# Value projection of a hybrid decoder trunk: a weight's two parts as one moving operand of 512 columns

## The chip, the cores and the metric

The kernel runs on one core of a Trainium2 chip. The metric is the device time of one execution in microseconds; a smaller time is better. The times below are medians over several executions, and the profile belongs to one execution of its own. Engines are named as in the profile: PE is TensorE's matmul and PEld its weight load, DVE is VectorE, ACT is ScalarE, POOL is GpSimd, and SP is SyncE, which issues most transfers.

## The reference

One layer of a decoder is computed on 1024 rows of 1024 columns: an RMS norm, two token mixers side by side (a gated linear recurrence, RG-LRU, and a gated linear attention with 8 heads, HGRN2), an output projection with residual, a second norm, a squared-ReLU MLP with residual, and a last norm. The part that matters here is the value projection of the second mixer:

```python
h = rms_norm(x, norm_mix[l])
proj = h @ w_in
xa, ga, q, f, v, g, m_a, m_b = jnp.split(proj, SPLIT_POINTS, axis=-1)
...
vf = v.astype(jnp.float32).reshape(B_, S_, HG_HEADS, HG_DV)
o = rms_norm(hgrn2_chunkwise(qf, kf, log_f, vf), hg_norm)
...
x = x + hybrid_mixer(h, lower_bounds[l], ...)
h = rms_norm(x, norm_mlp[l])
x = x + jnp.square(jax.nn.relu(h @ w_up[l])) @ w_down[l]
```

## The kernel before

**Two parts of a number.** Products keep close to float32 precision because each operand is split in two: a rounded part (names ending in H) and the rest (names ending in L), both in the fp32r format. A cast on ACT makes the rounded part (L87), a subtraction on DVE the rest (L92). A product is then three matmuls into one PSUM bank, H by H, H by L and L by H; `mm3` issues them (L146 to L150).

**Stages.** The mixers work in eight stages: 2 chunks c of 512 rows times 4 pairs p of heads, named c0 p0 to c1 p3. `stage(i)` projects what pair i needs from the normalised rows: xa (the recurrence's input, with its convolution), q, f, and the recurrence's gates (`rg_lru`). The value projection of a pair is made one stage later: `stage(i+1)` begins with `v_of(i+1)`, which runs `v_steps` for pair i (L521 to L538). At the same time `hgrn(i)` (from L664) makes the scores and states of pair i. The two are interleaved by hand: `hgrn` calls `go(n)`, which lets the following stage go n steps on. The numbers come from the tables GO, GO_FIRST and GO_SECOND_HALF (L36 to L38). In most stages 22 steps come first (16 of them values), then the score product of level 1 (`pt1`, 32 small matmuls out of q1 and kk), 2 steps, that of level 2 (`pt2`, out of qa and kb), 2 steps, and that of level 8 (`pt8`). These three are recorded at L678; in the orders below they are sc1, sc2 and sc8.

**A value projection.** `v_steps` makes for each of four row tiles (tt, 128 rows) a sum over eight contraction tiles k. The rows' transposed parts hh and hl are the stationary operand of 128 by 128, and 256 columns of the weight are the moving operand. The result, 128 by 256 in PSUM, is copied to SBUF by ACT (L535) and is read much later (`po`, L870, and `pkv`, L845). After row tile 0, `between` runs the tail of the recurrence of the pair: its elementwise products and two scans along time on DVE (L627 to L631). The first pair's values, v_00, are made elsewhere (`first_norm`, L382 to L397).

**PSUM banks.** Eight banks are given out by tag in turn: "pj" has four, "sc" two, "hg" two. Row tiles 0, 1 and 3 of the values take a "pj" bank, row tile 2 an "sc" bank. The turn of "sc" in a stage is: the gates' second half (pr and pi), the values' row tile 2, sc1, sc2, and later the product sc64. So sc2 takes the bank of row tile 2. In the turn of "pj" the three value tiles are followed by xa's two banks and q's two; xa's second bank takes that of row tile 0, and q's two take those of row tiles 1 and 3.

**Weights.** `next_w` hands out weights in a fixed sequence. A weight's H and L are two tiles of 128 by 1024 of the tag "w", of which there are six: three weights are held at a time. `split_w` fills them; on a weight's second use the rest is loaded back from DRAM. `pair` in the MLP takes tiles of the same ring.

**Order of the work.** PE's matmuls of the mixers are kept in program order (`pin`). On DVE and ACT the scheduler sets the order of the instructions from its own estimates, except where the code says otherwise (`keep`, `high_priority`).

**After the mixers.** The output projection follows (`out_proj`), then the MLP, as block products with fewer multiplications by a plan of sums (PLAN, from L1059). Between its up and down halves DVE forms sums of weight blocks (L1089 to L1098), rests (L92) and the squared-ReLU input (L1530).

Of the kernel before, what the change touches and what calls it, by code (L numbers as in the profile page):

```python
# [11 lines left out]
F32R = mybir.dt.float32r  # L12
U8 = mybir.dt.uint8
AF = mybir.ActivationFunctionType
ALU = mybir.AluOpType
# [3 lines left out]
P = 128  # L19
# [26 lines left out]
def trunk(ctx: ExitStack, tc: tile.TileContext, x, wts, mlp, pv, gains, mask_f, mask_u, out):  # L46
    nc = tc.nc
    V, A, G, PE = nc.vector, nc.scalar, nc.gpsimd, nc.tensor

    const = ctx.enter_context(tc.tile_pool(name="const", bufs=1))  # L50
    wp = ctx.enter_context(tc.tile_pool(name="wp", bufs=1))
# [30 lines left out]
    def keep(ins):  # L82
        if in_order[0]:
            tc.keep_in_program_order(ins)
# [14 lines left out]
    def load_w(i):  # L99
        raw = raw_tile(f"raw{i}")  # L100
        nc.sync.dma_start(raw, seq[i])
        return raw

    def split_w(i, raw):
        if i < n_mix + 3:
            h, lo = (wp.tile([P, 1024], F32R, tag="w", name=f"w{q}{i}", bufs=6) for q in "HL")
        else:
            h, lo = (kept[0].tile([P, 1024], F32R, tag=f"k{q}{i - n_mix}", name=f"w{q}{i}") for q in "HL")
        at = pair_tiles[i] if i < len(pair_tiles) else None
        with tc.high_priority(400):  # L110
            if at in rests:
                A.copy(h, raw)  # L112
                nc.sync.dma_start(lo.bitcast(F32), rests[at])
                return h, lo
            split(raw, h, lo)
        if at is not None and at in pair_tiles[i + 1 :]:
            rests[at] = dram.tile([P, 1024], F32, tag=f"rest{at}", name=f"rest{at}")
            nc.sync.dma_start(rests[at], lo.bitcast(F32))
        return h, lo
# [10 lines left out]
    def get_w(i, ahead=2):  # L130
        fill_w(i + ahead + 1)
        return ready.pop(i)

    used = [0]

    def next_w():
        used[0] += 1
        return get_w(used[0] - 1)
# [3 lines left out]
    def pin(ins):  # L142
        if pinned[0]:
            tc.keep_in_program_order(ins)

    def mm3(o, ah, al, bh, bl, first, last, goes_on=False):  # L146
        how = {"skip_group_check": True} if goes_on else {}
        pin(PE.matmul(o, ah, bh, start=first, stop=False, **how))  # L148
        pin(PE.matmul(o, ah, bl, start=False, stop=False, **how))  # L149
        pin(PE.matmul(o, al, bh, start=False, stop=last, **how))  # L150
# [75 lines left out]
    def mt(tag, name, shape=(P, T), dt=F32, bufs=1):  # L226
        return m.tile(list(shape), dt, tag=tag, name=name, bufs=bufs)
# [65 lines left out]
    def first_norm():  # L293
# [73 lines left out]
        ws, pv = {}, {}  # L367

        def w_high(i):
            ws[i] = tuple(wp.tile([P, 1024], F32R, tag="w", name=f"w{q}{i}", bufs=6) for q in "HL")  # L370
            keep(A.copy(ws[i][0], xraws[i]))

        def w_low(i):
# [6 lines left out]
        v = mt("v", "v_00", (P, 4, 256))  # L380
# [139 lines left out]

    def v_steps(c, p, got, between):  # L521
        v = mt("v", f"v_{c}{p}", (P, 4, 256))
        w = [next_w(), next_w()]
        for tt in range(4):
            pp = bank("sc" if tt == 2 else "pj", f"pv_{c}{p}_{tt}")
            for k in range(8):
                hh, hl = kt(hT[c], k)
                cut = slice(tt * P, (tt + 1) * P)
                cols = slice((k % 4) * 256, (k % 4 + 1) * 256)
                wh, wl = w[k // 4]  # L530
                mm3(pp[:, :256], hh[:, cut], hl[:, cut], wh[:, cols], wl[:, cols], k == 0, k == 7)
                if k % 2:
                    if k < 7:
                        yield
            A.copy(v[:, tt, :], pp[:, :256])  # L535
            between(tt)
            yield
        got["v"] = v  # L538
# [540 lines left out]
    def quad_steps(i, pools, raws=raw_tile, minus=False):  # L1079

        ops = ops_w[i] = {}
        s = []

        def sums(behind=None):
            ra, rb = (r.rearrange("p (a b) -> p a b", a=2) for r in raw_q[i])
            a11, a21, a12, a22 = ra[:, 0, :], ra[:, 1, :], rb[:, 0, :], rb[:, 1, :]
            s.extend(raws(f"s{i}{h}") for h in range(2))
            sa, sb = (r.rearrange("p (a b) -> p a b", a=2) for r in s)
            ins = V.tensor_tensor(out=sa[:, 0, :], in0=a21, in1=a22, op=ALU.add)  # L1089
            if behind is not None:  # L1090
                how = mybir.DependencyInfo(mybir.DependencyClass.NoSync, mybir.DependencyReason.DATA)
                tc.add_manual_dep(ins.ins, behind.ins.name, how, reason="sums")
            if minus:
                V.scalar_tensor_tensor(sa[:, 1, :], sa[:, 0, :], -1.0, a11, op0=ALU.mult, op1=ALU.subtract)
            else:
                V.tensor_tensor(out=sa[:, 1, :], in0=sa[:, 0, :], in1=a11, op=ALU.add)
            V.tensor_tensor(out=sb[:, 0, :], in0=a21, in1=a11, op=ALU.add)  # L1097
            V.tensor_tensor(out=sb[:, 1, :], in0=a12 if minus else sa[:, 1, :], in1=sa[:, 1, :] if minus else a12, op=ALU.subtract if minus else ALU.add)  # L1098

        def single(behind=None):  # L1100
            t = pools[0].tile([P, 2, 512], F32R, tag="w1", name=f"wA11{i}", bufs=2)
            split(raw_q[i][0][:, 0:512], t[:, 0, :], t[:, 1, :], behind)
            ops["A11"] = (t[:, 0, :], t[:, 1, :])

        def pair(src, names):
            def go(pool=None, tag=None, bufs=None):
                if pool:
                    t = pool.tile([P, 2, 1024], F32R, tag=tag, name=f"w{names[0]}{i}", bufs=bufs)
                    h, lo = t[:, 0], t[:, 1]
                else:  # L1110
                    h, lo = (pools[1].tile([P, 1024], F32R, tag="w", name=f"w{names[0]}{i}{q}", bufs=6) for q in "HL")
                split(src(), h, lo)
                for j, o in enumerate(names):
                    cols = slice(j * 512, (j + 1) * 512)
                    ops[o] = (h[:, cols], lo[:, cols])

            return go

        return {
            "sums": sums,  # L1120
            "a": single,
            "b": pair(lambda: s[0], ("s1", "s2")),
            "c": pair(lambda: s[1], ("s3", "s4")),
            "d": pair(lambda: raw_q[i][1], ("A12", "A22")),
        }
# [9 lines left out]
    for o in ("t1", "n2", "T4", "T3"):  # L1135
        pool = np_ if o in ("t1", "n2") else tp
# [315 lines left out]
    for part in range(2):  # L1452
# [4 lines left out]
        for hf in range(2):  # L1457
            pp = {tt: bank("pj", f"po1{hf}{tt}") for tt in tts}
# [3 lines left out]
            for n, (j, those) in enumerate(turn):  # L1462
                if n == 4:
                    first_weights()
                wh, wl = out_w[4 * hf + j]
                for k in range(2):
                    ku = 2 * j + k
                    yh, yl = ykt1(part, ku)
                    cols = slice(k * 512, (k + 1) * 512)
                    for tt in those:  # L1470
                        cut = slice((tt % 2) * P, (tt % 2 + 1) * P)
# [3 lines left out]
            for tt in tts:  # L1475
                cols = slice(hf * 512, (hf + 1) * 512)
# [176 lines left out]
    for kb in range(n_kb):  # L1653
        last = kb + 1 == n_kb
        qs = order[2 * kb : 2 * kb + 2]
        for half in range(2):
# [8 lines left out]
            for step, (bk, wo, uo), prs in [  # L1665
# [3 lines left out]
                for i, q in enumerate(qs):  # L1669
                    wh, wl = ops_w[QUADS + q][wo]  # L1670
                    uh, ul = u_ops[q][uo]
                    for pr in prs:
                        if first and i == 0:
                            banks[bk, pr] = bank(BANK[bk], f"d{bk}{kb}{pr}")
                        cut = slice(pr * P, (pr + 1) * P)
                        mm3(banks[bk, pr], uh[:, cut], ul[:, cut], wh, wl, first and i == 0, i == 1, not first)
                for pr in prs:
                    _, ci, cj, op = ADDS[step]
# [92 lines left out]
```

## Time and profile before

| | us |
|---|---|
| median of 3 runs | 1538.94 (1538.2 to 1539.3) |
| the profiled execution | 1538.52 |
| its span, first to last instruction | 1536.7 |
| PE busy | 1522.4 (99%) |
| DVE busy | 1149.0 (75%) |
| ACT busy | 804.6 (52%) |
| POOL busy | 153.6 (10%) |
| mean granted PE clock | 0.998 |

A row of a timeline reads: start in us from the span's start, duration in us, engine, line, operation, output <- inputs (by the program's names, without buffer numbers), shapes, and in brackets the idle time of the engine just before it with what ended it. A row with "x64" is 64 instructions drawn together. A row of waits reads: the waiting engine, tile and line, what it waited for, and then us in total, the number of times, and the longest. A row of a group gives the shortest, median and longest duration in ns, and the first and last start. Matmuls overlap one another, so their pace is read from the distance of their starts.

### The profile page before, as it was taken

The page shows a single profiled execution, that of the slowest core. Times are in us where ns is not written, and L with a number is a line of the kernel's source. Part 1 is how long each engine was busy: PE and PEld are TensorE (multiplying, and loading weights), DVE is VectorE, ACT ScalarE, POOL GpSimd, SP SyncE. Part 2 cuts the span into 40 slices and gives each one's busy share as a digit, 9 for nine tenths or more (in the row PEclk, how much of TensorE's full clock was granted, in tenths as well). Part 3 has the DMA queues.
Part 4 walks back from the last instruction along what each step waited for, and adds up shares of the span by engine and source line. Part 5 has one row for each costly group of instructions (what it writes and reads, how often), then busy time and mean ns, then how long its engine had stood idle before and what let it go on. Part 6 is the DMA issues. An engine that isn't in the chain of part 4 may idle for free. (4 is left out here: it accounts for less than half of the span.)

```text
span 1536.7 us, 23202 instructions
## 1 busy us (share of the span) xinstructions
PE 1522.4 (99%) x9085; PEld 1275.2 (83%) x9085; DVE 1149.0 (75%) x1656; ACT 804.6 (52%) x1341; POOL 153.6 (10%) x188
## 2 busy tenths in 40 slices
PE   9999999999999999999999999999999999999997
PEld 7878988889889888888888888888888788888886
DVE  6798695485675838786856578888888898888877
ACT  6646757567567335454533447666666721111115
POOL 1022210232624600000000000000000000000000
PEclk9999999999999999999999999999999999999999
DMA  8545455465674274432338324666666685666642
GB/s 298 200 153 193 150 193 200 147 217 174 224 232 140 99 298 165 151 137 83 137 106 329 127 110 161 261 251 249 249 253 247 229 308 223 249 252 251 250 182 110
DMA packets 81679, 306.82 MB, mean 200 GB/s; under 512 B 8481, under 2 KB 20897, under 8 KB 68642
## 3 DMA queue, kind: packets, MB, share of 16 engines
q1 hardware_dynamic: 77536, 292.75, 52.0%
q10 hardware_dynamic: 4034, 12.59, 2.1%
q8 instruction: 71, 1.16, 0.3%
q14 instruction: 38, 0.31, 0.1%
HBM read 201.50 MB, written 103.81 MB: 199 GB/s over the span
## 5 line engine op out<-in xcount | busy, mean ns | idle before, releaser
L1680 DVE TENSOR_TENSOR acc<-acc,dX 128x512 f32<-128x512 f32 x128 | 85.3, 686 | 28.2 <-PE dX L150 27.8
L87 ACT CAST wA<-q 128x512 fp32r<-128x512 f32 x46 | 28.5, 620 | 136.1 <-PE dX L150 101.6
L92 DVE TENSOR_TENSOR wL<-raw,wH 128x1024 fp32r<-128x1024 f32 x46 | 56.3, 1226 | 40.7 <-ACT wH L87 39.8
L87 ACT CAST wH<-raw 128x1024 fp32r<-128x1024 f32 x46 | 48.2, 1049 | 33.8 <-DMA raw<-wts_in 14.9
L1680 DVE TENSOR_TENSOR acc<-acc,dY 128x512 f32<-128x512 f32 x64 | 43.5, 687 | 13.3 <-PE dY L150 13.1
L148 PE MATMUL po<-wH,y 128*128 128x512 f32 x128 | 49.9, 393 | 0.0
L149 PE MATMUL po<-wL,y 128*128 128x512 f32 x128 | 49.9, 389 | 0.0
L150 PE MATMUL po<-wH,y 128*128 128x512 f32 x128 | 49.7, 390 | 0.0
L1531 ACT ACTIVATE b<-b 128x512 f32<-128x512 f32 x48 | 30.0, 625 | 29.2 <-DVE b L1530 29.0
L92 DVE TENSOR_TENSOR wA<-q,wA 128x512 fp32r<-128x512 f32 x46 | 31.5, 687 | 15.2 <-ACT wA L87 15.1
L112 ACT CAST wH<-raw 128x1024 fp32r<-128x1024 f32 x36 | 37.7, 1047 | 8.3 <-issue 3.7
L179 POOL TENSOR_TENSOR rstd_h<-rstd_h,mhalf 128x1 f32<-128x1 f32 x8 | 4.6, 583 | 370.8 <-DVE rstd_h L174 370.8
L573 DVE SCALAR_TENSOR_TENSOR xc<-xp,pvt,xc 128x512 f32<-128x512 f32 x48 | 40.2, 849 | 1.1 <-ACT xc L557 1.1
L1089 DVE TENSOR_TENSOR s<-q,q 128x512 f32<-128x512 f32 x46 | 31.7, 688 | 4.4 <-DMA q<-mlp_in 4.0
L486 POOL TENSOR_TENSOR stt<-r,stt 128x256 fp32r<-128x256 f32 x16 | 19.8, 1260 | 126.4 <-ACT stt L485 114.2
L1097 DVE TENSOR_TENSOR s<-q 128x512 f32<-128x512 f32 x46 | 31.6, 687 | 0.2
L1532 ACT ACTIVATE b<-b 128x512 f32<-128x512 f32 x48 | 30.1, 630 | 1.0
L877 ACT ACTIVATE on<-po 128x128 f32<-128x128 f32 x64 | 16.8, 277 | 26.1 <-PE po L873 26.0
L150 PEld LDWEIGHTS po<-wH,y 128*128 128x128 f32 x128 | 24.0, 188 | 5.0
L149 PEld LDWEIGHTS po<-wL,y 128*128 128x128 f32 x128 | 24.1, 188 | 4.8
L148 PEld LDWEIGHTS po<-wH,y 128*128 128x128 f32 x128 | 24.0, 188 | 4.8
L1179 DVE TENSOR_TENSOR gb<-gY,ge 128x512 f32<-128x512 f32 x14 | 9.7, 691 | 23.7 <-PE gY L150 23.7
(2562 smaller groups left out, 5439.1 us busy)
## 6 DMA issues: line engine op xcount, KB each, us to landing
q<-mlp_in SPq DMA_DIRECT2D x92, 512.0 KB, 3.7
raw<-wts_in SPq DMA_DIRECT2D x80, 512.0 KB, 5.0
rest<-wL SPq DMA_DIRECT2D x36, 512.0 KB, 2.9
wL<-rest SPq DMA_DIRECT2D x36, 512.0 KB, 4.3
hd<-ri SPq DMA_DIRECT2D x16, 256.0 KB, 3.5
od<-onT ACTq DMA_DIRECT2D x8, 512.0 KB, 6.6
cdT<-stT SPq DMA_DIRECT2D x16, 256.0 KB, 3.2
o<-od SPq DMA_DIRECT2D x4, 1024.0 KB, 7.2
```

The costliest lines, as they stand in the source:

```text
L87: ins = A.copy(h, src)
L92: ins = V.tensor_tensor(out=lo, in0=src, in1=h.bitcast(F32), op=ALU.subtract)
L112: A.copy(h, raw)
L148: pin(PE.matmul(o, ah, bh, start=first, stop=False, **how))
L149: pin(PE.matmul(o, ah, bl, start=False, stop=False, **how))
L150: pin(PE.matmul(o, al, bh, start=False, stop=last, **how))
L573: ins = V.scalar_tensor_tensor(xc[:, s, :], xp[:, j : j + T], pvt[:, PV_CW + 8 * j + u : PV_CW + 8 * j + u + 1], xc[:, s, :], op0=ALU.mult ...
L1089: ins = V.tensor_tensor(out=sa[:, 0, :], in0=a21, in1=a22, op=ALU.add)
L1097: V.tensor_tensor(out=sb[:, 0, :], in0=a21, in1=a11, op=ALU.add)
L1531: A.activation(b[:, at, :], b[:, at, :], AF.Relu, scale=-1.0 if at == 2 else 1.0)
L1532: A.activation(b[:, at, :], b[:, at, :], AF.Square)
L1680: V.tensor_tensor(out=dst, in0=dst, in1=banks[bk, pr], op=op)
```

## The change

A weight's two parts now lie in one tile of 2 by 1024 columns, which `w_pair` allocates; there are three of these in place of six single ones. `both_parts` keeps the whole tile under the weight's name. In `v_steps` the two matmuls with the stationary operand hh become one: its moving operand is 2 by 256 columns, out of both parts, with a distance of 1024 columns between the runs, and its result fills the whole bank, H by H in the first half and H by L in the second. The third matmul, L by H, adds 256 columns to the first half. Afterwards ACT copies the second half to SBUF, and a new DVE instruction adds the first half from PSUM to it. This concerns the seven pairs of `v_steps`, not the first.

```diff
+    both_parts = {}
+
+    def w_pair(pool, name):
+        t = pool.tile([P, 2, 1024], F32R, tag="w", name=name, bufs=3)
+        both_parts[name] = t
+        return t[:, 0, :], t[:, 1, :]
+
     def split_w(i, raw):
         if i < n_mix + 3:
-            h, lo = (wp.tile([P, 1024], F32R, tag="w", name=f"w{q}{i}", bufs=6) for q in "HL")
+            h, lo = w_pair(wp, f"w{i}")
...
         def w_high(i):
-            ws[i] = tuple(wp.tile([P, 1024], F32R, tag="w", name=f"w{q}{i}", bufs=6) for q in "HL")
+            ws[i] = w_pair(wp, f"w{i}")
...
     def v_steps(c, p, got, between):
         v = mt("v", f"v_{c}{p}", (P, 4, 256))
-        w = [next_w(), next_w()]
+        w = [(both_parts[f"w{used[0]}"], next_w())[0] for _ in range(2)]
         for tt in range(4):
             pp = bank("sc" if tt == 2 else "pj", f"pv_{c}{p}_{tt}")
             for k in range(8):
                 hh, hl = kt(hT[c], k)
                 cut = slice(tt * P, (tt + 1) * P)
                 cols = slice((k % 4) * 256, (k % 4 + 1) * 256)
-                wh, wl = w[k // 4]
-                mm3(pp[:, :256], hh[:, cut], hl[:, cut], wh[:, cols], wl[:, cols], k == 0, k == 7)
+                both = w[k // 4][:, :, cols]
+                pin(PE.matmul(pp.rearrange("p (a b) -> p a b", a=2), hh[:, cut], both, start=k == 0, stop=False))
+                pin(PE.matmul(pp[:, :256], hl[:, cut], both[:, 0, :], start=False, stop=k == 7))
                 if k % 2:
                     if k < 7:
                         yield
-            A.copy(v[:, tt, :], pp[:, :256])
+            A.copy(v[:, tt, :], pp[:, 256:])
+            V.tensor_tensor(out=v[:, tt, :], in0=pp[:, :256], in1=v[:, tt, :], op=ALU.add)
             between(tt)
             yield
...
-                    h, lo = (pools[1].tile([P, 1024], F32R, tag="w", name=f"w{names[0]}{i}{q}", bufs=6) for q in "HL")
+                    h, lo = w_pair(pools[1], f"w{names[0]}{i}")
```

Lines move by 7 up to `v_steps` and by 9 behind it: the scan of L631 is L640 in the changed kernel, the products of L668 are L677, the subtraction of L1530 is L1539; the new add is L544.

The change also alters the scheduler's order. On DVE in stage c0 p2, around the second scan of the recurrence (ri02), before; sc1_02 is the level-1 score product, whose masked copy goes to dd02:

```order
L631 SCALAR_TENSOR_TENSOR ri02_1913<-a02_1915,hcar_126,ri02_1913 128x512
L92 TENSOR_TENSOR hT10L_89<-xT_x13_0_2246,hT10H_88 128x4x128
L92 TENSOR_TENSOR hT11L_87<-xT_x13_1_2253,hT11H_86 128x4x128
L668 TENSOR_TENSOR qb02_2016<-qb02_2016,seg02_2009 128x32x2x8
L631 SCALAR_TENSOR_TENSOR ri02_1913<-a02_1915,hcar_126,ri02_1913 128x512
L668 TENSOR_TENSOR seg02_2009<-seg02_2009 128x32 x2
L668 TENSOR_TENSOR dd02_2007<-sc1_02_2260,mf_121 128x256
```

and the same place on DVE in the changed kernel:

```order
L640 SCALAR_TENSOR_TENSOR ri02_1858<-a02_1860,hcar_126,ri02_1858 128x512
L677 TENSOR_TENSOR qb02_1961<-qb02_1961,seg02_1954 128x32x2x8
L640 SCALAR_TENSOR_TENSOR ri02_1858<-a02_1860,hcar_126,ri02_1858 128x512
L544 TENSOR_TENSOR v_02_1979<-pv_02_1_2022,v_02_1979 128x256
L544 TENSOR_TENSOR v_02_1979<-pv_02_2_2055,v_02_1979 128x256
L544 TENSOR_TENSOR v_02_1979<-pv_02_3_2074,v_02_1979 128x256
L677 TENSOR_TENSOR seg02_1954<-seg02_1954 128x32 x2
L677 TENSOR_TENSOR dd02_1952<-sc1_02_2173,mf_121 128x256
```

The adds of row tiles 1, 2 and 3 stand together behind the second scan and ahead of the masked copy; that of row tile 0 stands earlier, between the clamp of f and the first product with f. The stages c0 p3 to c1 p3 have the same order. In the last stage, c1 p3, DVE had this before:

```order
L631 SCALAR_TENSOR_TENSOR ri13_5401<-a13_5403,hcar_126,ri13_5401 128x512
L668 TENSOR_TENSOR qb13_5517<-qb13_5517,seg13_5510 128x32x2x8
L631 SCALAR_TENSOR_TENSOR ri13_5401<-a13_5403,hcar_126,ri13_5401 128x512
L668 TENSOR_TENSOR seg13_5510<-seg13_5510 128x32 x2
L668 TENSOR_TENSOR dd13_5508<-sc1_13_5746,mf_121 128x256
```

and has this now:

```order
L640 SCALAR_TENSOR_TENSOR ri13_5161<-a13_5163,hcar_126,ri13_5161 128x512
L677 TENSOR_TENSOR qb13_5277<-qb13_5277,seg13_5270 128x32x2x8
L640 SCALAR_TENSOR_TENSOR ri13_5161<-a13_5163,hcar_126,ri13_5161 128x512
L544 TENSOR_TENSOR v_13_5295<-pv_13_1_5332,v_13_5295 128x256
L544 TENSOR_TENSOR v_13_5295<-pv_13_2_5365,v_13_5295 128x256
L544 TENSOR_TENSOR v_13_5295<-pv_13_3_5384,v_13_5295 128x256
L677 TENSOR_TENSOR seg13_5270<-seg13_5270 128x32 x2
L677 TENSOR_TENSOR dd13_5268<-sc1_13_5474,mf_121 128x256
```

Here nothing but the three adds comes in. Between the MLP's up and down halves, DVE had this order, where b14 and b15 are the squared-ReLU inputs, q and s the weight blocks and their sums:

```order
L1098 TENSOR_TENSOR s301_11277<-s300_11276,q301_11259 128x512
L1068 TENSOR_TENSOR b14_11086<-b14_11086 128x512
L92 TENSOR_TENSOR wA1131_11416<-q310_11406,wA1131_11416 128x512
...
L92 TENSOR_TENSOR ws130L_11286<-s300_11276,ws130H_11285 128x1024
L92 TENSOR_TENSOR ws131L_11420<-s310_11410,ws131H_11419 128x1024
...
L92 TENSOR_TENSOR wA1231L_11428<-q311_11407,wA1231H_11427 128x1024
L1530 TENSOR_TENSOR b15_11240<-uZ15_11289,e0_15_11241 128x512
L1530 TENSOR_TENSOR b15_11240<-uX15_11227,e1_15_11256 128x512
```

and has this now:

```order
L1077 TENSOR_TENSOR b14_10724<-b14_10724 128x512
L92 TENSOR_TENSOR wA1131_11048<-q310_11038,wA1131_11048 128x512
...
L1107 TENSOR_TENSOR s301_10912<-s300_10911,q301_10894 128x512
...
L92 TENSOR_TENSOR wA1231_11057<-q311_11039,wA1231_11057 128x1024
L92 TENSOR_TENSOR u14n2_10859<-b14_10724,u14n2_10859 128x1024
L92 TENSOR_TENSOR ws130_10920<-s300_10911,ws130_10920 128x1024
L1539 TENSOR_TENSOR b15_10875<-uZ15_10923,e0_15_10876 128x512
L1539 TENSOR_TENSOR b15_10875<-uX15_10862,e1_15_10891 128x512
```

The sum s301 went from ahead of the rest of wA1131 to behind it, and the rest of ws130 from the first of the rests to the last of them. In the first stage, c0 p0, the last two state updates sn00 (L856, now L865) stood ahead of the product kb01 on DVE, and now stand behind it.

## The prediction

> **What bounds the kernel now.** I read the busy times and the slices first, then the waits of the tensor engine (PE) and after them the timeline at each place where the change adds a wait.
>
> ```profile
> PE 1522.4 (99%) x9085; PEld 1275.2 (83%) x9085; DVE 1149.0 (75%) x1656; ACT 804.6 (52%) x1341; POOL 153.6 (10%) x188
> PEclk9999999999999999999999999999999999999999
> ```
>
> PE works 1522.4 us of a span of 1536.7, at a granted clock that is full in all 40 slices. So the program is as long as PE's own work, and every stall of PE is paid in full. The waits say how little it stalls.
>
> ```profile
> PE gain L318 <- POOL gain_row L308: 2.5, 1, 2.5
> PE dZ L148 <- ACT wA1230H L87: 1.0, 1, 1.0
> PE po L870 <- DVE sn L856: 0.9, 1, 0.9
> PE uX L148 <- DVE b L1530: 0.5, 1, 0.5
> ```
>
> The first belongs to the start, and no other is over 1 us. VectorE (DVE) has a quarter of the span free on average, but an average doesn't tell whether it is on time where PE will ask for it. Two questions follow: how much PE work goes, and where do the new adds of DVE make PE wait.
>
> **Matmuls taken away.** The rows show PE passing from 512-column matmuls to the value products' 256-column ones.
>
> ```profile
> 299.68 0.39 PE L150 MATMUL pj_f<-hT11H,wL 128*128 128x512 f32 x1
> 303.08 0.39 PE L150 MATMUL pj_f<-hT11H,wL 128*128 128x512 f32 x1
> 303.42 0.28 PE L149 MATMUL pv<-wL,hT10H 128*128 128x256 f32 x1
> 308.94 0.28 PE L150 MATMUL pv<-wH,hT11L 128*128 128x256 f32 x1
> ```
>
> Between the first two lie 15 steps, (303.08 - 299.68) / 15 = 0.2267 us each; between the last two 46 steps, (308.94 - 303.42) / 46 = 0.1200. Three of 256 took 0.3600; one of 512 and one of 256 take 0.3467. The multiplied columns are the same 768: what goes is one fixed cost per product, 2 x 0.1200 - 0.2267 = 0.0133 us. Seven pairs x 4 row tiles x 8 contractions are 224 products: **-2.99 us**, 32 x 0.0133 = 0.43 us in each stage.
>
> The Trainium skill ("TensorE: Matmul & The Clock Gate", Part 1, "Wait — 56ns, not 53.3ns?") gives a warm matmul only about 2.5 ns beyond its columns; by that the change would save an estimated 0.56 us. The rows above disagree, with 13.3 ns, and decide.
>
> That a 512-column operand gathered from two runs, 4 KB apart, streams like a contiguous one isn't shown by any row. Loss bound: the whole saving, 2.99 us. I exclude a gain beyond it, since the columns stay, and take the full saving, the row's own pace for that size.
>
> **The adds on DVE.** Each value row tile now has a copy on ScalarE (ACT) as before, and an add on DVE behind it.
>
> ```profile
> L535 ACT COPY v<-pv x28: 352/374/422, 125.9 to 502.6; 128x256 f32<-128x256 f32 x28
> L668 DVE TENSOR_TENSOR dd<-sc,mf x8: 411/421/432, 88.3 to 514.1; 128x256 f32<-128x256 f32 x8
> ```
>
> The copy keeps its size. For the add, the nearest row is the product from PSUM and SBUF of the same size: 0.42 us to its end. 28 of them at a pitch of 0.35 (below) are 9.8 us of DVE, free wherever DVE has room. But the bank of row tile 2 is of the tag "sc", and the next-but-one user of that bank is sc2, the level-2 score product (L678, out of qa and kb). PE runs in order, so sc2 and all behind it now wait for the add of row tile 2 instead of a copy. The three adds of row tiles 1 to 3 stand on DVE directly behind the second recurrence scan. So I compare, in each stage, when DVE leaves the second scan and when PE gets to sc2. Stage c0 p2:
>
> ```profile
> 186.70:206.20 19.50, 19.50 (x233) 16.83 (x232) 19.47 (x30) 13.23 (x23) 0.19 (x1) 1.00 0.54 193
> 204.96 1.29 DVE L631 TENSOR_TENSOR_SCAN ri<-a,hcar,ri 128x512 f32<-128x512 f32 x1
> 206.16 0.33 DVE L668 TENSOR_TENSOR seg<-seg 128x32 f32<-128x32 f32 x2
> 206.39 0.43 DVE L668 TENSOR_TENSOR dd<-sc,mf 128x256 f32<-128x256 f32 x1
> 206.72 0.35 DVE L668 TENSOR_TENSOR seg<-seg 128x32 f32<-128x32 f32 x2
> 204.96 0.89 PE L678 MATMUL sc<-qa,kb 128*32 128x48 f32 x64
> 194.03 0.38 ACT L535 COPY v<-pv 128x256 f32<-128x256 f32 x1
> ```
>
> The first row is a window (length; then busy PE, PEld, DVE, ACT, POOL): DVE worked 19.47 of 19.50 us. It has no room, so the add of row tile 0, which stands in this stretch, pushes the scan by its pitch; the 256-wide product started at 206.39 and the next operation at 206.72, 0.33, and I use 0.35. DVE left the scan at 206.16. The add of row tile 2 ends at 206.16 + 0.35 (tile 0) + 0.35 (tile 1) + 0.42 = 207.28. PE came to sc2 at 204.96, now 0.43 earlier, 204.53. **Stall: 2.75 us.** Row tile 2's copy was done by 194.41, so in the kernel before the bank was long free. In short, the stall is 0.35 + 0.35 + 0.42 + 0.43 = 1.55 us minus what sc2 lies behind DVE's release, here 1.55 + 1.20.
>
> Four stages, c0 p3 to c1 p2, look alike; the first and the last of them:
>
> ```profile
> 263.56 1.08 DVE L668 TENSOR_TENSOR seg<-seg 128x32 f32<-128x32 f32 x7
> 266.33 0.89 PE L678 MATMUL sc<-qa,kb 128*32 128x48 f32 x64
> 267.29 0.45 DVE L697 COPY_PREDICATED dd<-mu,sc 128x192 f32<-128x192 uint8 x1 [1.84 <-PE sc L678]
> 447.27 1.09 DVE L668 TENSOR_TENSOR seg<-seg 128x32 f32<-128x32 f32 x7
> 450.05 0.89 PE L678 MATMUL sc<-qa,kb 128*32 128x48 f32 x64
> ```
>
> There sc2 lies 2.77 and 2.78 us behind DVE's release, over the 1.55 needed, with 1.2 to spare; and the 1.40 us of adds go into DVE's idle 1.84 ahead of 267.29. Cost nothing; without that cover 1.40 each. The last stage, c1 p3:
>
> ```profile
> 494.00:512.00 18.00, 18.00 (x221) 15.46 (x220) 17.74 (x27) 12.80 (x24) 8.61 (x3) 1.00 0.21 74
> L631 DVE TENSOR_TENSOR_SCAN ri<-a,hcar,ri x16: 1274/1278/1772, 82.8 to 511.8; 128x512 f32<-128x512 f32 x16
> 513.42 0.81 DVE L668 TENSOR_TENSOR seg<-seg 128x32 f32<-128x32 f32 x2
> 511.24 0.89 PE L678 MATMUL sc<-qa,kb 128*32 128x48 f32 x64
> 503.39 7.89 POOL L486 TENSOR_TENSOR stt<-r,stt 128x256 fp32r<-128x256 f32 x2 [20.31 <-ACT stt L485]
> ```
>
> DVE is full again (17.74 of 18.00) and is free only at 513.42, 2.18 behind sc2: **stall 1.55 + 2.18 = 3.73 us.** Its scans took up to 1.772 against a median of 1.278, with GpSimd (POOL) at work beside them; that POOL is the cause is not shown. If both came back to the median, the stall would be 0.99 shorter, 2.7.
>
> **What the scheduler moves.** Where the sums of the weights are formed between the up and the down projection, two DVE steps change places:
>
> ```profile
> 1208.58 0.62 ACT L87 CAST wA<-q 128x512 fp32r<-128x512 f32 x1 [0.48 <-DMA q<-mlp_in]
> 1208.51 0.69 DVE L1068 TENSOR_TENSOR b<-b 128x512 f32<-128x512 f32 x1
> 1209.23 0.69 DVE L92 TENSOR_TENSOR wA<-q,wA 128x512 fp32r<-128x512 f32 x1
> 1213.45 1.22 DVE L92 TENSOR_TENSOR ws130L<-s,ws130H 128x1024 fp32r<-128x1024 f32 x1
> 1220.86 0.69 DVE L1530 TENSOR_TENSOR b<-uX,e 128x512 f32<-128x512 f32 x1
> 1221.60 0.50 PE L148 MATMUL uX<-h2T4H,wA1215H 128*128 128x512 f32 x1 [0.53 <-DVE b L1530]
> ```
>
> The wA rest at 1209.23 follows a cast that ended at 1209.20 and waited for a load. The sum s301 (L1098, 0.60 by pitch) stood ahead of it and now stands behind it: DVE waits first and works later. The rest of ws130 moves too, but stays ahead of L1530. PE at 1221.60 already waited for L1530, so **+0.6**; bounds 0 (an earlier load) and 1.2 (the moved rest, too).
>
> In the first stage the state updates sn change places with two products:
>
> ```profile
> 110.15 0.68 PE L870 MATMUL po<-v,scT 128*128 128x128 f32 x4 [0.94 <-DVE sn L856]
> 110.95 0.36 DVE L856 SCALAR_TENSOR_TENSOR sn<-sn,seg,pkv 128x128 f32<-128x128 f32 x1
> 111.78 0.61 PE L870 MATMUL po<-v,scT 128*128 128x128 f32 x4
> ```
>
> The last sn update ended at 111.31; a 0.6 us product now precedes it. PE's first wait of 0.94 shrinks, but the second half, begun at 111.78, waits to about 112.0: **+0.3** (between -0.45, the first wait alone, and +0.6). The other reorderings leave each result early enough for its reader: 0; their cover gone, they would act as the wait above does.
>
> The ring of weight tiles holds the same three pairs, freed together as they were: 0. No DMA is added, and none is moved past another.
>
> **The sum.** -2.99 + 2.75 + 3.73 + 0.6 + 0.3 = +4.39 us. The profiled execution took 1538.52; with this 1542.9. The median of the runs is 1538.94: **forecast 1543.3 us.**
>
> **Rivals.** About 0.2% (3.1 us) is what a measurement can tell from no change: faster means below 1535.9, slower above 1542.0.
> - Main case, both stalls, 0.54. Lower end: -2.99 + 2.75 + 2.7 + 0 - 0.45 = +2.0, 1540.9; upper: with an extra 0.35 in each stall, 1.2 and 0.6, +6.0, 1544.9.
> - One stall only, 0.19: DVE gets through c0 p2 or c1 p3 sooner, since its input, too, comes from PE. +1.64 or +0.66, 1539.6 to 1540.6. Against it: windows without a gap.
> - No stall, the other side, 0.12: DVE's release is early enough in all seven stages, which needs 1.2 to 2.2 us and the 1.55 gained. Then -2.99 stands against -0.45 to 0.9: 1535.5 to 1536.9, some two fifths of it under 1535.9. For it: the four stages with 1.2 to spare; against it: nothing leaves those two stretches.
> - The change doesn't save what it says, 0.11: the two-run operand costs its 0.0133 per product, +7.4, 1546.3.
> - The clock, 0.04: if a 3.73 us stall brought the clock to half for as long, half of 3.73 is lost behind it, +1.87, 1545.2. Against it: the slice with the 2.5 us wait shows full clock. The Trainium skill ("TensorE: Matmul & The Clock Gate", Part 1, "What's actually happening") names an idle window of about 3.4 us for such a drop; no wait here reaches it.
>
> **The numbers.** Slower is 0.44 of the main case, the unsaved matmuls and the clock, 0.59; faster two fifths of the no-stall case, 0.05; same the rest, 0.36. The range leaves the no-stall case out and reaches from below the one-stall cases, 1538.5, to the unsaved case with a little of the upper bounds, 1547.0.
>
> **What would show it.** Right: PE waits at sc2 for the new add in c0 p2 and c1 p3 alone, 2.8 and 3.7 us; a pace of 0.347 us per product; 28 adds of 0.42; the wait for L1530 at 1.1. Wrong: PE's busy time not 3 us down, sc2 waits in other stages or none, or the time below 1538.5.

## The result and the profile after

| | before | after |
|---|---|---|
| median, us | 1539.15 (6 runs, 1538.20 to 1539.62) | 1548.94 (6 runs, 1546.28 to 1551.98) |
| the profiled execution, us | 1538.52 | 1549.26 |
| its span, us | 1536.7 | 1547.5 |
| mean granted PE clock | 0.998 | 0.996 |

The ratio is 1.0066 (95% interval 1.0056 to 1.0076): 10.2 us slower, between 8.6 and 11.7. The forecast was 1543.3 with a range up to 1547.0. The sign and the two stalls held; the size did not, and what made most of the difference stood in no term of the sum.

The busy times of the profiled execution after the change:

```profile
PE 1525.2 (99%) x8861; PEld 1265.6 (82%) x8861; DVE 1152.0 (74%) x1684; ACT 802.8 (52%) x1341; POOL 152.0 (10%) x188
```

The 224 matmuls are gone from the count, 28 instructions have come to DVE. But PE's busy time rose by 2.8 us where it should have lost 3: the same work must have run slower somewhere. The waits of PE after the change:

```profile
PE sc L687 <- DVE v L544: 6.0, 2, 3.6
PE gain L325 <- POOL gain_row L315: 2.5, 1, 2.5
PE dZ L155 <- ACT wA L87: 1.0, 1, 1.0
PE xT_x L358 <- DVE xn L349: 0.9, 1, 0.9
PE dY L156 <- DVE ws L92: 0.7, 1, 0.7
...
PE uX L155 <- DVE b L1539: 0.5, 1, 0.5
```

The first row is the forecast stall: sc2 waits for the new add, twice and nowhere else. The timeline shows the two places, c0 p2 and c1 p3, with the group of three adds ahead of each:

```profile
207.99 1.05 DVE L544 TENSOR_TENSOR v<-pv,v 128x256 f32<-128x256 f32 x3
208.85 1.51 PE L687 MATMUL sc<-qa,kb 128*32 128x48 f32 x64 [2.32 <-DVE v L544]
517.95 1.05 DVE L544 TENSOR_TENSOR v<-pv,v 128x256 f32<-128x256 f32 x3
518.82 1.17 PE L687 MATMUL sc<-qa,kb 128*32 128x48 f32 x64 [3.65 <-DVE v L544]
```

2.32 and 3.65 us were forecast as 2.75 and 3.73. What was not forecast stands in the same rows: the 64 small matmuls of sc2 took 1.51 and 1.17 us; before, 0.89. The windows of 1 us around the two places (length, PE's busy time with its matmuls, then the granted clock, the DMA share and GB/s) show why:

```profile
206.00:207.00 1.00, 0.53 (x3) 1.00 0.20 74
207.00:208.00 1.00, 0.00 (x0) 1.00 0.68 258
208.00:209.00 1.00, 0.15 (x9) 0.83 0.13 53
209.00:210.00 1.00, 1.00 (x60) 0.50 0.62 238
210.00:211.00 1.00, 1.00 (x21) 0.50 0.00 0
211.00:212.00 1.00, 1.00 (x4) 0.50 0.43 180
212.00:213.00 1.00, 1.00 (x5) 0.97 1.06 344
...
518.00:519.00 1.00, 0.18 (x17) 1.00 0.74 262
519.00:520.00 1.00, 1.00 (x65) 0.63 0.23 83
520.00:521.00 1.00, 1.00 (x3) 0.50 1.09 407
521.00:522.00 1.00, 1.00 (x4) 0.50 0.93 297
522.00:523.00 1.00, 1.00 (x4) 0.66 0.00 0
```

Behind each wait PE ran at half clock, for 3.4 us. In windows of 0.1 us the first drop lies from 208.65 to 212.07, the second from 519.27 to 522.68.

Set side by side, matmul by matmul, the two timelines give the whole account. They are compared in the order of issue, since two matmuls of dY have moved behind three of dX at the handover from the up to the down projection. The offset of after against before is +0.64 us at the first transposes (loads that landed later), +1.90 at the end of the first stage, then +5.32 behind the stall of c0 p2, +9.16 behind that of c1 p3, +9.65 ahead of the handover (0.4 of this comes at one place of the up projection, near 971 us of before), +10.53 behind it, and +10.82 at the end. In the stages between it falls by 0.27 to 0.31 us each: that is the matmul saving. In the first merged stage it falls by 0.56, but 0.34 of that is no saving: the eight transposes among its values cost the kernel before 1.13 us to the next matmul's start, 124.76 to 125.89, and e2_ring_only (below), which merges no product either, 0.79, 125.12 to 125.91:

```profile
124.76 1.38 PE L546 MATMUL poT<-ident,on 128*128 128x128 f32 x8
125.12 1.04 PE L553 MATMUL poT<-ident,on 128*128 128x128 f32 x8
```

In all: 0.64 (start) + 0.92 (first stage) - 1.97 (matmuls, seven stages) + 0.46 (around the transposes ahead of c0 p2's stall) + 3.80 and 5.31 (the two stalls with what follows them) + 0.49 (from there to the handover) + 0.88 (handover) + 0.29 (behind it) = 10.8.

### The profile page after: what moved, and what is told of

It reads as the page before. It is cut to its first block, busy times and chain, and to the rows that moved or that the text cites. A ratio compares the mean times of both kernels' runs of the same rounds, so it can differ in the third digit from the quotient of the medians.

```text
span 1547.5 us, 22712 instructions
## 1 busy us (share of the span) xinstructions
PE 1525.2 (99%) x8861; PEld 1265.6 (82%) x8861; DVE 1152.0 (74%) x1684; ACT 802.8 (52%) x1341; POOL 152.0 (10%) x188
## 3 DMA queue, kind: packets, MB, share of 16 engines
q8 instruction: 69, 1.13, 0.3%
## 5 line engine op out<-in xcount | busy, mean ns | idle before, releaser
L87 ACT CAST ws<-s 128x1024 fp32r<-128x1024 f32 x92 | 96.2, 1049 | 113.9 <-PE dX L157 42.3
L87 ACT CAST wA<-q 128x512 fp32r<-128x512 f32 (+1 forms) x92 | 76.6, 835 | 144.8 <-PE dX L157 104.2
L92 DVE TENSOR_TENSOR ws<-s,ws 128x1024 fp32r<-128x1024 f32 x92 | 112.2, 1221 | 29.7 <-ACT ws L87 29.6
L92 DVE TENSOR_TENSOR wA<-q,wA 128x512 fp32r<-128x512 f32 (+1 forms) x92 | 87.3, 955 | 50.0 <-ACT wA L87 49.8
L92 DVE TENSOR_TENSOR w<-raw,w 128x1024 fp32r<-128x1024 f32 x41 | 50.1, 1228 | 33.4 <-ACT w L87 33.2
L87 ACT CAST w<-raw 128x1024 fp32r<-128x1024 f32 x41 | 42.9, 1048 | 22.9 <-issue 10.3
L1689 DVE TENSOR_TENSOR acc<-acc,dY 128x512 f32<-128x512 f32 x64 | 43.5, 685 | 13.5 <-PE dY L157 13.3
L119 ACT CAST w<-raw 128x1024 fp32r<-128x1024 f32 x36 | 37.6, 1045 | 17.4 <-PE pj_f L157 7.7
L1536 ACT COPY e<-uX 128x512 f32<-128x512 f32 x32 | 18.6, 583 | 29.8 <-PE uX L157 29.8
L156 PE MATMUL po<-wL,y 128*128 128x512 f32 x80 | 31.1, 389 | 0.0
L155 PE MATMUL po<-wH,y 128*128 128x512 f32 x80 | 31.0, 393 | 0.0
L157 PE MATMUL po<-wH,y 128*128 128x512 f32 x80 | 31.0, 389 | 0.0
L1185 ACT COPY ge<-gX 128x512 f32<-128x512 f32 x28 | 16.3, 584 | 26.8 <-PE gX L157 26.8
```

Source lines behind the costliest of these rows:

```text
L87: ins = A.copy(h, src)
L92: ins = V.tensor_tensor(out=lo, in0=src, in1=h.bitcast(F32), op=ALU.subtract)
L1689: V.tensor_tensor(out=dst, in0=dst, in1=banks[bk, pr], op=op)
```

## The experiments

**Theories.** A: each of the two waits is paid twice, as the wait and as half clock behind it; the rest is the exchanged steps. Rivals: the clock falls because of the wider matmuls (B); DVE's extra work makes PE late wherever the adds stand (C); GpSimd's work beside DVE is what makes the last stage late (D).

**The adds ahead of the scans.**

```diff
             A.copy(v[:, tt, :], pp[:, 256:])
-            V.tensor_tensor(out=v[:, tt, :], in0=pp[:, :256], in1=v[:, tt, :], op=ALU.add)
+            with tc.high_priority(400):
+                V.tensor_tensor(out=v[:, tt, :], in0=pp[:, :256], in1=v[:, tt, :], op=ALU.add)
```

> The changed kernel with one edit: the 28 adds have a high scheduling priority, so that they stand ahead of the recurrence scans on DVE. Theory A (each of the two waits at sc2 is paid twice, once as PE's wait and once as about 3.4 us at half clock behind it): both waits and both drops of the granted clock go, 2.32 + 3.65 + 2 x 1.7 = 9.4 us off the changed kernel's 1548.9, so 1539.5 (1538.5 to 1540.5), and the runs lie as close together as those of the kernel before. Rival B (the clock falls because of the wider matmuls, not because of the wait): the waits go, the drops stay, 1543. Rival C (the adds only move the delay, the scans come later and PE waits for the level-8 product instead): waits of 1 us and more at the next score product, 1541 to 1545.

Measured: 1547.38 us, ratio to before 1.0059 (1.0047 to 1.0072). The stall of c0 p2 and its drop are gone; in c1 p3 the wait moved to the level-8 product, as C and D have it:

```profile
506.69 0.92 DVE L678 TENSOR_TENSOR seg<-seg 128x128 f32<-128x128 f32 x1
504.44 2.93 POOL L493 TENSOR_TENSOR stt<-r,stt 128x256 fp32r<-128x256 f32 x2 [20.21 <-ACT stt L492]
516.92 1.74 DVE L641 TENSOR_TENSOR_SCAN ri<-a,hcar,ri 128x512 f32<-128x512 f32 x1
519.78 1.51 PE L688 MATMUL sc<-qb,kc 128*32 128x48 f32 x64 [4.12 <-DVE qb L678]
```

and the window of 20 us behind it:

```profile
520.00:540.00 20.00, 20.00 (x180) 0.85 0.20 71
```

A product of 128 columns on DVE took 0.92 us with GpSimd (POOL) at work beside it, and PE stood still for 4.12 us. The clock's mean fell to 0.85 in that window: the drop lasted twice as long as the others, from 519.11 to 525.94. By the offsets c1 p3 now costs 7.0 us in place of 5.3, which eats up much of what c0 p2 gained. The time is above what A (1539.5) and C (1541 to 1545) gave. So theory A stands for c0 p2, but the order of the adds does not cure c1 p3. B is out: in c0 p2 the wider matmuls stayed and the clock did not fall.

**GpSimd's work later.** On top of the adds first, five of GpSimd's steps are issued later:

```diff
-            combos_on(1 if i == 4 else 2)
+            combos_on({4: 1, 7: 0}.get(i, 2))
...
         yield from v_of(NC * NPAIR)
-        combos_on(2)
...
-            if c == 0:
-                combos_on(1)
+            if c == 1:
+                combos_on(5)
```

> As e1_adds_first, but GpSimd's sums of the last two pieces (five of their steps), which ran beside DVE's full stretch in c1 p3, are issued later, behind the second half of the projection g. In e1_adds_first PE waited 4.1 us at the level-8 score product of c1 p3 and DVE's small products took up to 0.9 us there in place of 0.4. If GpSimd's work slows DVE there: the scans of c1 p3 take 1.28 us, the wait at the level-8 product is under 0.5 us, no drop of the clock, and the time is the weight tile's +2.5 us less 7 x 0.30 us, so +0.4 us on the kernel before (0 to +1.5). Rival (the adds alone are too much for that stretch): a wait of 2 us or more remains there, with a drop behind it, +3 to +7.

Measured: 1547.70 us, 1.0059 (1.0046 to 1.0071). DVE's stretch in c1 p3 now runs at its usual pace, and neither sc2 nor the level-8 product waits:

```profile
507.02 0.38 DVE L678 TENSOR_TENSOR seg<-seg 128x128 f32<-128x128 f32 x1
511.80 1.27 DVE L641 TENSOR_TENSOR_SCAN ri<-a,hcar,ri 128x512 f32<-128x512 f32 x1
515.80 0.89 PE L688 MATMUL sc<-qb,kc 128*32 128x48 f32 x64
534.74 0.41 ACT L492 CAST stt<-r 128x256 fp32r<-128x256 f32 x1 [5.63 <-POOL r L482]
537.98 2.93 PE L855 MATMUL pkv<-v,kT 128*128 128x128 f32 x12 [3.48 <-ACT kT L850]
```

D is shown: with GpSimd elsewhere a scan takes 1.27 us in place of 1.74, and the same 128-column product 0.38 in place of 0.92, with all seven pairs' adds in place. The Trainium skill ("SBUF — State Buffer", "SBUF: two separate sides") says that a GpSimd operation and a DVE operation with two SBUF inputs lock each other out; the rows agree, and so does the add, which has one input in PSUM and took 0.42 us in both (at 505.52 in e1_adds_first, at 505.74 here). The time did not follow: ACT's casts of the moved sums waited for GpSimd (the row at 534.74), the copy kT behind them came late, and PE waited 3.48 us for it at pkv, with a drop behind it from 537.36 to 544.19. The price was moved, not saved.

**No add in the two full stages.** The values of c0 p2 and c1 p3 are made as before:

```diff
+                if (c, p) in ((0, 2), (1, 3)):
+                    mm3(pp[:, :256], hh[:, cut], hl[:, cut], both[:, 0, :], both[:, 1, :], k == 0, k == 7)
+                else:
...
+            if (c, p) in ((0, 2), (1, 3)):
+                A.copy(v[:, tt, :], pp[:, :256])
+            else:
```

> The changed kernel, with the values of c0 p2 and c1 p3 made as before (three matmuls of 256 columns, a copy, no add), the other five pairs as in the change. Theory A (the two stages in which DVE has no room carry the loss, as PE's wait and as half clock behind it): no wait at sc2, clock full, and what is left is the new weight tile's 2.5 us (e2_ring_only) less five stages' 0.30 us, +1.0 us on the kernel before. Rival (the loss sits in the exchanged steps or in the wider matmuls of every stage): at least 4 us above the kernel before. Rival D (in c1 p3 DVE is late from GpSimd's work beside it, add or no add): a wait of 2 to 4 us at one of the score products of c1 p3 remains, +4 to +7.

Measured: 1540.71 us, 1.0010 (1.0001 to 1.0019): 1.5 us above before, of the change's 10.2. PE's longest wait there, of those at the scores, is the one that the kernel before has as well, and the granted clock is full from 12 to 1533.4 us:

```profile
PE sc L824 <- DVE qf L683: 0.5, 1, 0.5
12.00:1533.40 1521.40, 1513.33 (x8893) 1.00 0.54 199
```

and sc2 of c0 p2 starts without a wait:

```profile
206.51 0.89 PE L693 MATMUL sc<-qa,kb 128*32 128x48 f32 x64
```

Two of seven stages carry almost all of the loss: 8.7 us by the ratios, where the offsets gave 9.1, less the 0.6 that these two stages no longer save. In c1 p3 the scans still took 1.76 us beside GpSimd, without a wait of PE behind them: it takes both, GpSimd's work and the adds, to make DVE late there.

**Filling the wait.** To part the wait from the clock, PE works through matmuls that nobody reads while it would wait for sc2's bank; sc2 still starts when the add is done.

```diff
+        hh, _ = kt(hT[c], 0)
+        n_fill = {(0, 2): 10, (1, 3): 15}.get((c, p), 0)
+        if n_fill:
+            spare = bank("hg", f"fill{nm}")
+            for _ in range(n_fill):
+                pin(PE.matmul(spare, hh[:, :P], hh, start=True, stop=True))
         pt2 = blocks(kb, ...
```

> The changed kernel with matmuls whose result nobody reads ahead of sc2, 10 in c0 p2 and 15 in c1 p3, 0.227 us each, so that PE works while it would wait. Theory A (the waits halve the clock behind them): sc2 starts when it did, the waits are down to 0.1 to 0.4 us, both drops of the clock are gone, 2 x 1.7 = 3.4 us off the changed kernel, 1545.5, and its runs lie closer together. Rival (the clock falls because of what runs there, not because PE stood still): the drops stay, 1548.9.

Measured: 1547.24 us (1544.80 to 1548.43), 1.0051 (1.0037 to 1.0065). The clock stays full at both places and from 12 to 1539.9 us:

```profile
209.00:210.00 1.00, 1.00 (x53) 1.00 0.40 152
520.00:521.00 1.00, 1.00 (x7) 1.00 0.33 117
12.00:1539.90 1527.90, 1518.90 (x8854) 1.00 0.54 198
```

In its timeline the offset against before grows by 2.41 us across c0 p2's place and by 3.79 across c1 p3's, against 3.80 and 5.31 in the changed kernel: the drops cost 1.4 and 1.5, 2.9 us in all. The difference of the two ratios, 2.3 us, is of that size, but its uncertainty is as large. The expected 3.4 came out lower. In c0 p2 PE still waited for the first 0.2 us of the half clock; in c1 p3 it worked through all of it, and why that drop cost less than 1.7 is not shown. The runs still scatter, by 3.6 us over five against 5.7 over six of the changed kernel, so the clock does not make all of it. It makes a part: of the changed kernel's six executions the two with a mean clock of 0.998 took 1546.28 and 1546.50 us, the three with 0.996 took 1549.26 to 1551.98.

**Filling half of it.** 4 and 8 such matmuls in place of 10 and 15.

> As e7_filled_wait with 4 and 8 such matmuls, which leaves waits of about 2.32 - 0.91 = 1.4 us in c0 p2 and 3.65 - 1.82 = 1.8 us in c1 p3. Waits of 0.95 us had no drop behind them and one of 2.06 us that fell into one window had, so this narrows it: if any wait over 1 us halves the clock, two drops; if it takes 2 us within a window, none, and the time of e7_filled_wait.

One execution: 1547.90 us, with waits of 1.42 and 1.85 us left:

```profile
PE sc L687 <- DVE v L544: 3.3, 2, 1.8
```

The clock, over the program and in one window of 3.41 us:

```profile
12.00:1540.80 1528.80, 1516.24 (x8847) 1.00 0.54 198
516.85:520.26 3.41, 2.38 (x71) 1.00 0.64 226
```

No drop behind either. For the second wait that says less than it seems. If the clock goes by windows that run by themselves (the next experiment), they can be counted back in steps of 3.413 us from the half clock at this run's end, which begins at 1540.85. On that grid the wait of 1.42 us lies in one window, and it takes more than that; the wait of 1.85 us, 516.03 to 517.88, falls into two windows, 0.82 us in one and 1.03 in the next.

**Doses of waiting.** Multiplications by one in a chain ahead of the add of row tile 2, in four stages; in c0 p2 and c1 p3 the adds go first.

```diff
+            dose = {(0, 3): 8, (1, 0): 12, (1, 1): 16, (1, 2): 22}.get((c, p), 0)
+            if tt == 2:
+                for _ in range(dose):
+                    V.tensor_scalar(v[:, tt, :], v[:, tt, :], 1.0, None, op0=ALU.mult)
+            with tc.high_priority(400 if (c, p) in ((0, 2), (1, 3)) else 0):
+                V.tensor_tensor(out=v[:, tt, :], in0=pp[:, :256], in1=v[:, tt, :], op=ALU.add)
```

> The changed kernel with the adds first in the stages c0 p2 and c1 p3 (no wait there), and in the stages c0 p3, c1 p0, c1 p1 and c1 p2 with 8, 12, 16 and 22 extra DVE multiplications by one ahead of the add of row tile 2, so that PE waits at sc2 for four different times. Theory A (a free-running window of 3.41 us: the clock is halved for the next window when PE was idle in more than some part of one): a drop behind each wait of 2.2 us or more that falls for the most part into one window, none behind a short one, each drop 3.4 us long and all starts on one grid of 3.413 us. Rival (the clock falls behind any wait over a fixed length, at once and for as long as the wait lasted): drops that start when the wait reaches that length and last as long as the wait.

One execution: 1560.35 us. The design failed: sc2 waited 0.9 us in each of the four stages, whatever the dose. It started right behind the masked copy of sc1, as if it had been given sc1's bank, which was not checked. But the added work made PE wait elsewhere, and these waits serve as doses:

```profile
PE pk L849 <- DVE kk L682: 5.1, 3, 2.1
PE sc L692 <- DVE qb L682: 4.2, 1, 4.2
PE sc L692 <- DVE v L547: 3.7, 4, 0.9
```

Two of the waits at pk are as good as equal, 2.08 us up to 415.92 and 2.06 us up to 481.73. The windows are on the grid of 3.413 us through the drop at 483.06:

```profile
411.38:414.79 3.41, 2.45 (x11) 1.00 0.11 44
414.79:418.20 3.41, 2.28 (x14) 1.00 0.95 334
418.20:421.61 3.41, 3.41 (x26) 1.00 0.90 329
479.64:483.05 3.41, 1.35 (x10) 1.00 0.65 191
483.05:486.47 3.42, 3.42 (x15) 0.50 0.93 359
```

The first of the two falls into two windows, 0.96 and 1.13 us, and has no drop behind it; the second falls into one, and the clock fell at 483.06, 1.3 us after PE had gone back to work. Behind the wait of 4.2 us (527.87 to 532.05) it was half from 530.84 to 537.67, and began before the wait had ended. A drop that starts when a wait reaches some length does not do that; a window that runs by itself does.

**The new weight tile alone.** H and L in one tile, the value projection as before, no add.

```diff
-            h, lo = (wp.tile([P, 1024], F32R, tag="w", name=f"w{q}{i}", bufs=6) for q in "HL")
+            h, lo = w_pair(wp, f"w{i}")
...
     def v_steps(c, p, got, between):
         v = mt("v", f"v_{c}{p}", (P, 4, 256))
         w = [next_w(), next_w()]
```

> The kernel before with the new weight tile alone (H and L in one tile of 2 by 1024, three of them); the value projection is as it was, three matmuls of 256 columns, no add. Its order on DVE has the same exchanged steps in the first stage and between the MLP's halves as the changed kernel. Theory A with the exchanged steps as a cost of their own: no wait at sc2, clock full, 1.0 to 2.0 us above the kernel before, 1540.2 to 1541.2, with the steps at the same two places of the program as in the changed kernel. Rival (the exchanged steps cost nothing, what the trace of the changed kernel shows there is scatter): within 0.5 us of the kernel before, 1538.6 to 1539.6.

Measured: 1540.70 us, 1.0016 (1.0007 to 1.0025), 2.5 us slower, above the 1.0 to 2.0 expected. Its clock is full. The offset against before falls to -0.63 in the first norm, rises by 0.70 in the first stage, by 0.4 at the place of the up projection named above and by 0.50 at the handover, and ends at 1.48. So the tile by itself costs, though it adds no instruction. The profiled execution, 1539.92, is the fastest of the eleven; where the last 1 us of the 2.5 lies is not shown.

**The same, in the old order.** Three dependencies put kb behind the last state update, the rest of wA1131 behind s301 and the rest of ws131 behind ws130 (`how` stands for a kind of dependency that only orders):

```diff
+        if c + p == 1:
+            tc.add_manual_dep(ins.ins, gots[0]["states"].ins.name, how, reason="order")
...
+            if i == 31:
+                tc.add_manual_dep(ins.ins, order_w[30, "s"].ins.name, how, reason="order")
...
+                if (i, names[0]) == (31, "s1"):
+                    tc.add_manual_dep(ins.ins, order_w[30, "s1"].ins.name, how, reason="order")
```

> As e2_ring_only, with the same three dependencies that put the exchanged DVE steps back. If the exchanged steps are what e2_ring_only lost: 1.8 us faster than e2_ring_only and within 0.8 us of the kernel before, and its trace runs level with that of the kernel before through the first stage and between the MLP's halves. If the tile itself costs the time: as e2_ring_only, 2.5 us above the kernel before.

Measured: 1540.62 us, 1.0016 (1.0007 to 1.0025), as without them. In its trace the first stage costs 0.3 us in place of 0.7, but the handover 0.50 as in e2_ring_only: PE no longer waits at dY, but 1.0 us for the squared-ReLU input b in place of 0.5. The steps on DVE that I had named are not the handover's cause. ACT's queue shows another exchange:

```profile
1203.64 0.57 ACT L1549 ACTIVATE b<-uX 128x512 f32<-128x512 f32 x1
1204.11 1.03 ACT L87 CAST wA<-q 128x1024 fp32r<-128x1024 f32 x1
1205.05 0.63 ACT L1550 ACTIVATE b<-b 128x512 f32<-128x512 f32 x1
1205.71 1.05 ACT L87 CAST u14B<-b 128x1024 fp32r<-128x1024 f32 x1
```

The cast of a weight block (1204.11) has slipped in between two steps of the squared ReLU, and the cast of u14B, for which DVE's queue waits, comes behind it. In the kernel before, the weight's cast stood ahead of both steps (at 1202.15, the steps at 1203.09 and 1203.71). Whether this is what the handover costs was not tried.

**Old order with the adds first and GpSimd later.** The three dependencies on top of e10_adds_first_pool_later.

> As e10_adds_first_pool_later, and the exchanged DVE steps are put back in the order of the kernel before by dependencies that only order them: kb behind the last state update in the first stage, the rest of wA1131 behind the sum s301, the rest of ws131 behind that of ws130. If the exchanged steps cost what e2_ring_only's trace shows (0.8 us in the first stage, 1.0 us between the MLP's halves), 1.8 us faster than e10_adds_first_pool_later, 1.4 us (0.1%) faster than the kernel before. If they cost nothing: as e10_adds_first_pool_later.

Measured: 1546.19 us, 1.0051 (1.0038 to 1.0064), 1.5 us better than without them by the medians, 1.2 by the ratios, within the scatter of both; it keeps the wait of 3.5 us at pkv. In the two profiled executions the half clock behind that wait lasted 6.8 us there and 3.4 here, which alone is a difference of this size. No version here beats the kernel before. By the terms measured, an estimate, even one without any stall would not: -2.0 us for the matmuls against +2.5 for the tile.

**What the operand of 512 columns saves.** On top of e5_plain_in_two_stages, three matmuls of 256 columns in the five other stages, with the adds (a first form of this on top of e1_adds_first, e3_three_matmuls_adds_first, gave no result):

```diff
-                    pin(PE.matmul(pp.rearrange("p (a b) -> p a b", a=2), hh[:, cut], both, start=k == 0, stop=False))
+                    pin(PE.matmul(pp[:, :256], hh[:, cut], both[:, 0, :], start=k == 0, stop=False))
+                    pin(PE.matmul(pp[:, 256:], hh[:, cut], both[:, 1, :], start=False, stop=False, skip_group_check=True))
```

> As e5_plain_in_two_stages, but in the five merged stages each product is three matmuls of 256 columns, into the two halves of the bank, with the copy and the add. The difference to e5_plain_in_two_stages is what the operand of 512 columns saves. As forecast, 160 x 13.3 ns: 2.1 us slower. As the trace of the changed kernel shows it, 0.30 us in each of five stages: 1.5 us slower. If an operand of two runs saved nothing: the same time.

Measured: 1540.91 us, 1.0015 (1.0006 to 1.0024), against 1540.71 and 1.0010: 0.2 to 0.8 us slower, which the scatter doesn't tell from nothing nor from 1.5. By the offsets the saving is there, 0.3 us in a merged stage, while this kernel's offset stays level from stage to stage; but e5_plain_in_two_stages gave part of it back in the first merged stage, where PE, now early, waits 0.7 us for the normalised outputs.

## Why the prediction was wrong

- **The two stalls** (2.75 and 3.73): right in place and cause and near in size, 2.32 and 3.65. The four like stages had the forecast cover and no wait; none showed in any kernel that kept the change's order. The seventh, c0 p1, was not named in the forecast and had none either.
- **The clock**: the step that failed. The sum had nothing for it; it was a rival with a chance of 0.04, tied to the 3.73 us stall alone. I held against it the slice with the 2.5 us wait at the start, and the idle window of about 3.4 us that the prediction names, which no wait was said to reach, though the stall of 3.73 in the same item is longer. Both waits were enough, and each cost about 1.4 to 1.5 us behind it: 2.9 us. The slices were no evidence. A digit of 9 means 90% or more, and 3.4 us at half clock leave 0.96 of a slice of 38.4; the last slice of the kernel before is a 9 with half clock from 1531.06 on in it. Nor does the start show a full clock: there four matmuls of 256 columns took 0.85 us from start to start (10.39 to 11.24), against 0.48 a little later (14.99 to 15.47), and the profile prints 1.00 for both:

```profile
1498.20:1536.60 38.40, 30.73 (x135) 0.93 0.29 110
10.39 1.05 PE L390 MATMUL pv<-wL,hT00H 128*128 128x256 f32 x4
14.99 0.64 PE L390 MATMUL pv<-wH,hT00H 128*128 128x256 f32 x4
```

- **The matmuls** (-2.99): too large; 2.0 us came. In c1 p0's values the first matmuls of row tiles 0 and 1 start at 308.34 and 311.15, so that a product took 2.81 / 8 = 0.351 us; by the same count 0.354 in row tile 1 and 0.347 in row tile 3, where 0.3467 was forecast for all. The values of that stage take 11.96 us from first to last start (308.34 to 320.30) and took 12.25 (303.31 to 315.56), 0.29 us in place of 0.43. The 13.3 ns that a matmul costs beside its columns came in full in row tile 3 alone. That the two runs of the operand are the reason is not shown; all four tiles have them.
- **What the scheduler moves** (+0.6 and +0.3): too small. The first stage grew by 0.9 us, the handover by 0.9, and 0.5 ahead of it and 0.3 behind it stood in no term. The wait for L1530 was forecast at 1.1 us and stayed at 0.5; instead PE waited 0.7 us at dY for the rest of ws130, the step that was held to be early enough. The tile alone, without any change to the value projection, was measured at +2.5 us where I had taken it for 0. Putting the DVE steps back (e12_ring_order_held) did not make the handover cheaper; what makes it dearer stays open.
- **The last stage's scans**: left open in the forecast, and now shown to be GpSimd's doing.
- The start, 0.64 us, is when the first loads landed, in this one execution. The 0.46 around the transposes is not explained.

In the sum: -2.0 (matmuls) + 6.0 (waits) + 2.9 (clock) + 0.9 (first stage) + 1.7 (handover, with what lies ahead of it and behind it) + 0.6 (start) + 0.5 (around the transposes) make 10.6, against 10.7 between the two profiled executions. The clock is the largest term that the forecast lacked, but not the only one: with it alone the forecast would have been 1546.2.

## What to carry to other kernels

Where the tensor engine is the bound, price a wait of about 2 us or more as the wait plus a chance of half clock behind it, 1.4 to 1.5 us here, and look for it in short windows, since an average hides it. The chance is real: a wait of 2.06 us had it and one of 2.08 had not. Before a step is put on an engine with free time on average, read that engine's windows at the place where its result is asked for: two full stretches of seven cost more than the five others gained. A change of tiles alone can reorder a scheduler's program; measure it by itself.

## What the runs showed of the hardware

- The starts of the two drops in the changed kernel lie 310.6 us apart, 91 times 3.413, those in e4_doses 47.79 us, 14 times. Seen on such a grid, the windows ahead of a drop held 2.06 us (e4_doses), 2.12 (the changed kernel), 2.87 (e10_adds_first_pool_later), 2.89 (e11_order_held), 2.97 (the changed kernel and e4_doses) and 3.41 us (e1_adds_first) of standing still. Waits of 0.95 (e4_doses), 1.42 (e8_half_filled_wait) and 1.56 us (e11_order_held, up to 580.22) had no drop behind them, nor had the waits of 1.85 and 2.08 us that fell into two windows each. The Trainium skill ("TensorE: Matmul & The Clock Gate", Part 1, "What's actually happening") has the free-running window of about 3.4 us, and the runs agree; it asks for a whole idle window, and here about 60% of one was enough, while 46% was not.
- A drop lasted one window where PE worked through it or stood still for no more than 0.20 us of it (the changed kernel), and two where PE still stood still for 0.61, 0.67 or 1.21 us of the first (537.36 to 544.19 in e10_adds_first_pool_later, 519.11 to 525.94 in e1_adds_first, 530.84 to 537.67 in e4_doses).
- A DVE product of two SBUF operands took up to 0.92 us beside GpSimd against 0.38 without it, a scan 1.74 against 1.27, the add with a PSUM operand 0.42 in both (e1_adds_first, e10_adds_first_pool_later).
